# Rotary embedding on one core: the pieces of a tile dealt to the partitions in another order

## The chip, the core and the metric

The kernel runs on one core of a Trainium2 chip. The metric is the device time of one execution in microseconds (us), lower is better. A core has five engines: TensorE (PE), VectorE (DVE), ScalarE (ACT), GpSimd (POOL) and SyncE (SP). Data moves between the large memory (DRAM) and the on-chip SBUF through 16 DMA engines, which the queues of ACT and SP feed here. SBUF has 128 partitions.

## The reference

`x` is 16 x 512 x 1024 in fp32 (33.5 MB): 16 batches, 512 positions, 16 heads of 64. `cos` and `sin` are 512 x 32, one row for each position.

```python
x = x.reshape(batch, seq, num_heads, head_dim)
x1, x2 = x[..., :half_dim], x[..., half_dim:]
cos, sin = cos[None, :, None, :], sin[None, :, None, :]
rotated = np.concatenate([x1 * cos - x2 * sin, x1 * sin + x2 * cos], axis=-1)
```

Every element of `x` is read once and every element of the output is written once. Each row of 1024 is multiplied by its position's cos, its swapped halves by (-sin, sin), and the two products are added.

## The kernel before

**Tiles.** There are ten. Batches 0, 1, 14 and 15 are "singles" (2 MB: 512 rows, four on each partition, `R1 = 4`), and the other twelve batches go as six "pairs" (4 MB: 1024 rows, eight on each partition, `R2 = 8`). What a partition takes of a tile is one contiguous run of rows, a *piece*: 16 KB in a single, 32 KB in a pair. In a single, partition p holds piece p. In a pair, partition 2s+b holds the piece s of batch b of the pair, so that neighbouring partitions are a batch (2 MB) apart in DRAM. One DMA loads a tile and one stores it, from the same SBUF place: `x_sb` is a ring of 40 rows for each partition (five pairs, 20 MB in all) and results overwrite the input.

**Tables.** The cos and sin tables come in by two small DMAs to `stage`, four positions on each partition. For singles this is the right order as it is: DVE copies cos to PSUM (L264), and ACT writes (-sin, sin) to `s1_sb` (L182, L183). For pairs, partition 2s+b needs the eight positions of piece s. Two matmuls (L208) make that from `stage` with two selection matrices `pick`, which ACT cuts from an identity matrix in one ACTIVATE (L177); ACT writes the pairs' (-sin, sin) to `s2_sb` (L186, L187).

**Queues.** ACT issues all loads (L153): tile 0, the tables (L174), tile 1 and four pairs at once, without a wait, and the remaining four when the stores that free their place in the ring have landed. SP issues a store (L161) when the last row of a tile is done.

**Rows.** Each of the 64 rows u of a partition (1024 elements) is worked on in turn. GpSimd multiplies the swapped row by sin into `t2_sb` (L257; for six rows DVE does it, L286). DVE multiplies the row by cos into PSUM, `t1_ps` (L293). Then either DVE adds the two to `x_sb` (L304), or PE adds the product in PSUM with an identity matmul (L224) and ACT copies the sum to `x_sb` (L191), as a fixed list (`PE2`) says. Semaphores count rows: `sem_p` GpSimd's products, `sem_m` DVE's, `sem_v` and `sem_a` finished rows. The first GpSimd multiply waits for `s1_sb` and tile 0; GpSimd's first row of a pair waits for `s2_sb`.

Of the kernel before, what the change touches and what calls it, by code (L numbers as in the profile page):

```python
# [6 lines left out]
def bass_split_heads_rope_kernel(  # L7
# [16 lines left out]
    batch, seq, dim = x.shape  # L24
# [3 lines left out]
    P = 128  # L28
    R1 = seq // P
    R2 = 2 * R1  # L30
    assert R1 * P == seq and R1 == 4 and batch % 2 == 0

    fp32 = mybir.dt.float32
# [3 lines left out]
    COPY = mybir.ActivationFunctionType.Copy  # L37
# [9 lines left out]
    EARLY = (NU - RING) // R2  # L47
# [20 lines left out]
    with ExitStack() as stack:  # L68
        x_sb = stack.enter_context(nc.sbuf_tensor([P, RING, H, 2, HALF], fp32))
        t2_sb = stack.enter_context(nc.sbuf_tensor([P, NT2, H, 2, HALF], fp32))  # L70
        stage = stack.enter_context(nc.sbuf_tensor([P, 2, R1 * HALF], fp32))
        s1_sb = stack.enter_context(nc.sbuf_tensor([P, R1, 2, HALF], fp32))
        s2_sb = stack.enter_context(nc.sbuf_tensor([P, R2, 2, HALF], fp32))
        ident = stack.enter_context(nc.sbuf_tensor([P, P], fp32))
        pick = stack.enter_context(nc.sbuf_tensor([P, 2, P // 2, 2], fp32))
        zero = stack.enter_context(nc.sbuf_tensor([P, BANK], bf16))
        tab_ps = stack.enter_context(nc.psum_tensor([P, BANK], fp32))
        pair_ps = stack.enter_context(nc.psum_tensor([P, 2, 2, R1, HALF], fp32))
# [1 line left out]
        sem_in = [stack.enter_context(nc.semaphore(f"in{t}")) for t in range(NT)]  # L80
        sem_out = [stack.enter_context(nc.semaphore(f"out{k}")) for k in range(EARLY)]
        sem_rest = stack.enter_context(nc.semaphore("rest"))
# [11 lines left out]
        sem_g = stack.enter_context(nc.semaphore("pick"))  # L94
# [9 lines left out]
        def s_of(t, r):  # L104
            return s1_sb[:, r] if tiles[t][1] == R1 else s2_sb[:, r]

        x1 = x.rearrange("b (s r) d -> b s (r d)", r=R1)
        o1 = out.rearrange("b (s r) h d -> b s (r h d)", r=R1)
        x2 = x.rearrange("b (s r) d -> s b (r d)", r=R2)
        o2 = out.rearrange("b (s r) h d -> s b (r h d)", r=R2)  # L110
        xs = x_sb[:].rearrange("p n h t d -> p n (h t d)")

        def in_dram(single, pairs, t):
            b, n = tiles[t]
            return single[b] if n == R1 else pairs[:, b:b + 2, :]

        def in_sbuf(t):
            b, n = tiles[t]
            k = b * R1 % RING
            return x_sb[:, k:k + n].rearrange("p n h t d -> p (n h t d)")  # L120

        def where(u):
            t, r = rows[u]
            return t, r, u % RING
# [7 lines left out]
        def wait_added(eng, u):  # L132

            if n_pe[u]:
                eng.wait_ge(sem_a, n_pe[u])
            if n_comb[u]:
                eng.wait_ge(sem_v, n_comb[u])
# [10 lines left out]
        def stores_of(k):  # L148

            return sum(b * R1 // R2 == k for b, _ in tiles)  # L150

        def load(eng, t):
            eng.dma_start(in_sbuf(t), in_dram(x1, x2, t)).then_inc(sem_in[t], 16)  # L153

        def on_sync(sp):
            for u in range(NU):
                t, r, k = where(u)
                if r == tiles[t][1] - 1:
                    wait_added(sp, u)
                    k = u // R2  # L160
                    sp.dma_start(in_dram(o1, o2, t), in_sbuf(t)).then_inc(sem_out[k] if k < EARLY else sem_rest, 16)  # L161
            sp.wait_ge(sem_rest, 16 * sum(stores_of(k) for k in range(EARLY, NU // R2)))

        def on_scalar(ae):
            later = {}
            for t, (b, n) in enumerate(tiles):
                if b * R1 + n <= RING:
                    load(ae, t)
                else:

                    later.setdefault((b * R1 - RING) // R2 * R2 + R2 - 1 + LAG, []).append(t)
                if t == 0:
                    for i, (table, sem) in enumerate(((cos, sem_cos), (sin, sem_sin))):
                        ae.dma_start(stage[:, i, :], table.rearrange("(s r) d -> s (r d)", r=R1)).then_inc(sem, 16)  # L174

            ae.wait_ge(sem_i, 2)
            ae.activation(  # L177
                pick[:], ident[:].rearrange("q (s k) -> q k s", k=2)[:, :, :, None].broadcast_to([P, 2, P // 2, 2]), COPY
            ).then_inc(sem_g, 1)
            ae.wait_ge(sem_sin, 16)  # L180
            sv = stage[:, 1, :].rearrange("s (r d) -> s r d", d=HALF)
            ae.activation(s1_sb[:, :, 0, :], sv, COPY, scale=-1.0)  # L182
            ae.activation(s1_sb[:, :, 1, :], sv, COPY).then_inc(sem_s, 1)  # L183
            ae.wait_ge(sem_t, 2)
            s2 = s2_sb[:].rearrange("p (k r) t d -> p k r t d", r=R1)
            ae.activation(s2[:, :, :, 0, :], pair_ps[:, :, 1, :, :], COPY, scale=-1.0)  # L186
            ae.activation(s2[:, :, :, 1, :], pair_ps[:, :, 1, :, :], COPY).then_inc(sem_s, 1)  # L187
            for u in range(NU):
                if PE2[u]:
                    ae.wait_ge(sem_e, n_pe[u])  # L190
                    ae.activation(xs[:, u % RING, :], t1_ps[:, u % NT1, :], COPY).then_inc(sem_a, 1)  # L191
                for t in later.get(u, ()):
                    k = (tiles[t][0] * R1 - RING) // R2
                    ae.wait_ge(sem_out[k], 16 * stores_of(k))
                    load(ae, t)

        def on_tensor(pe):
            pe.wait_ge(sem_z, 1)
            for k in range(NT1):
                for b in range(EH):  # L200
                    pe.matmul(  # L201
                        t1_ps[:, k, b * BANK:(b + 1) * BANK], zero[:, 0:P], zero[:], start=True, stop=True
                    ).then_inc(sem_w, 1)
            pe.wait_ge(sem_g, 1)
            pe.wait_ge(sem_cos, 16)
            pe.wait_ge(sem_sin, 16)
            for k in range(2):
                pe.matmul(  # L208
                    pair_ps[:, k].rearrange("p c r d -> p (c r d)"),
                    pick[:, k].rearrange("q s b -> q (s b)"),  # L210
                    stage[:].rearrange("q c f -> q (c f)"),
                    start=True,
                    stop=True,
                ).then_inc(sem_t, 1)
            for u in range(NU):
                if not PE2[u]:
                    continue
                pe.wait_ge(sem_m, u + 1)

                if not V2[u]:  # L220
                    pe.wait_ge(sem_p, n_pool[u])
                t2 = t2_sb[:, u % NT2, :, :, :].rearrange("p h t d -> p (h t d)")
                for b in range(EH):
                    ins = pe.matmul(  # L224
                        t1_ps[:, u % NT1, b * BANK:(b + 1) * BANK],
                        ident[:],
                        t2[:, b * BANK:(b + 1) * BANK],
                        start=False,
                        stop=True,
                        skip_group_check=True,  # L230
                    )
                ins.then_inc(sem_e, 1)
# [28 lines left out]
        def on_vector(ve):  # L261
# [49 lines left out]
            for u in range(NU + LEAD):  # L311
                if u < NU:
                    mul(u)
                if u >= LEAD and not PE2[u - LEAD]:
                    comb(u - LEAD)

        on_sync(nc.sync)
        on_scalar(nc.scalar)
        on_gpsimd(nc.gpsimd)
        on_tensor(nc.tensor)  # L320
        on_vector(nc.vector)

# [32 lines left out]
```

## Time and profile before

| what | value |
|---|---|
| median of 3 runs | 161.33 us (161.15 to 161.42) |
| span of the profiled execution, first to last instruction | 160.3 us |
| median of the runs less that span | 1.0 us |
| busy: POOL, DVE, PE, ACT | 134.9, 130.3, 72.8, 24.4 us |
| DMA | 67.26 MB, 419 GB/s over the span |
| load and store queues, share of 16 DMA engines' span | 49.6% and 48.9% |
| first load issued; first and last store issued | 0.8; 20.5 and 151.7 us |

The span is what the profile shows of one execution; the time of a run is about 1 us more, which lies around it. "Share of 16 engines" is the summed length of a queue's packets over 16 times the span. A row of a group gives busy time and the mean of one instruction, then the idle time before them and who ended it. ACTq and SPq are the issuing queues of ACT and SP: a DMA's row there is only its issue, and its packets follow later. The trace also records each DMA packet with its queue, start, length and size, but not which of the 16 DMA engines carried it.

### The profile page before, as it was taken

How to read it: one execution, taken by the hardware profiler on the slowest of the kernel's cores; microseconds unless marked ns; L12 is line 12 of the kernel's file. 1: busy time of each engine (PE TensorE's matmuls, PEld its weight loads, DVE VectorE, ACT ScalarE, POOL GpSimd, SP SyncE). 2: the span in 40 equal slices, each digit the busy share in tenths (PEclk: the TensorE clock that was granted, in tenths of full speed). 3: DMA queues.
4: the chain of work that ended last, by engine and by line, in shares of the span. 5: the costliest groups of instructions: out<-in, count | busy, mean ns of one | idle time of the engine just before them, and what ended most of it. 6: DMA issues, size and time to landing. Idle time of an engine off the chain costs nothing.

```text
span 160.3 us, 522 instructions
## 1 busy us (share of the span) xinstructions
PE 72.8 (45%) x94; PEld 24.0 (15%) x94; DVE 130.3 (81%) x117; ACT 24.4 (15%) x27; POOL 134.9 (84%) x64
## 2 busy tenths in 40 slices
PE   6050004478357936660847105489458435850000
PEld 1020002022202211210221002022202111220000
DVE  0069998599989999996999709899889999999500
ACT  0420000203120222022012010201220402040000
POOL 1059999999999999999999999699999999289400
PEclk9955555557755587689687965555555977699555
DMA  5999999999999999999999999999999999999896
GB/s 147 409 441 474 409 450 409 425 429 429 446 429 458 417 411 466 409 433 401 450 433 425 425 409 458 409 433 433 411 429 462 441 417 401 450 441 441 376 450 294
DMA packets 3170, 67.26 MB, mean 419 GB/s; under 512 B 352, under 2 KB 608, under 8 KB 608
## 3 DMA queue, kind: packets, MB, share of 16 engines
q10 hardware_dynamic: 1728, 33.69, 49.6%
q1 hardware_dynamic: 1440, 33.56, 48.9%
q14 instruction: 2, 0.02, 0.0%
HBM read 33.69 MB, written 33.55 MB: 419 GB/s over the span
## 4 chain that ended last, share of the span: by engine, by line
DMA 60%; POOL 13%; DVE 8%; PE 7%; issue 3%; ACT 2%; ACTq 1%; DVEq 0%
DMA x_sb<-in_x_dram 41%; DMA out_dram<-x_sb 18%; POOL t_sb L257 13%; PE t_ps L224 7%; DVE t_ps L293 5%; DVE x_sb L304 3%; ACT x_sb L191 2%; ACTq L153 1%; ACTq L174 1%; DVE t_sb L286 0%; DVEq L303 0%
## 5 line engine op out<-in xcount | busy, mean ns | idle before, releaser
L257 POOL TENSOR_TENSOR t_sb<-x_sb,s_sb 128x1024 f32<-128x1024 f32 x58 | 134.2, 2346 | 14.8 <-ACT s_sb L183 8.5
L224 PE MATMUL t_ps<-t_sb,ident 128*128 128x512 f32 x84 | 68.0, 957 | 63.0 <-DVE t_ps L293 39.2
L293 DVE TENSOR_TENSOR t_ps<-x_sb,pair_ps 128x1024 f32<-128x1024 f32 x48 | 57.7, 1223 | 9.9 <-ACT x_sb L191 9.8
L304 DVE TENSOR_TENSOR x_sb<-t_ps,t_sb 128x1024 f32<-128x1024 f32 x43 | 52.4, 1218 | 2.6 <-POOL t_sb L257 2.6
L224 PEld LDWEIGHTS t_ps<-t_sb,ident 128*128 128x128 f32 x84 | 22.1, 290 | 108.9 <-DVE t_ps L293 74.6
L191 ACT ACTIVATE x_sb<-t_ps 128x1024 f32<-128x1024 f32 x21 | 21.5, 1023 | 109.9 <-PE t_ps L224 96.9
L293 DVE TENSOR_TENSOR t_ps<-x_sb,tab_ps 128x1024 f32<-128x1024 f32 x16 | 19.3, 1222 | 0.1
L286 DVE TENSOR_TENSOR t_sb<-x_sb,tab_ps 128x1024 f32<-128x1024 f32 x6 | 7.3, 1213 | 0.0
L264 DVE COPY tab_ps<-stage 128x128 f32<-128x128 f32 x1 | 0.3, 294 | 7.8 <-DMA stage<-in_cos_dram 7.8
L208 PE MATMUL pair_ps<-stage,pick 128*128 128x256 f32 x4 | 2.0, 667 | 5.4 <-DMA stage<-in_sin_dram 5.4
L201 PE MATMUL t_ps<-zero 128*128 128x512 bf16 x6 | 2.7, 627 | 1.3 <-DVE zero L262 1.3
L208 PEld LDWEIGHTS pair_ps<-stage,pick 128*128 128x128 f32 x4 | 1.2, 324 | 6.4 <-issue 6.3
L177 ACT ACT_TABLE_LOAD x1 | 1.3, 1283 | 5.5 <-issue 5.5
L201 PEld LDWEIGHTS t_ps<-zero 128*128 128x128 bf16 x6 | 0.7, 136 | 2.4 <-DVE zero L262 1.2
L262 DVE MEMSET zero<- 128x256 uint32 x1 | 0.3, 272 | 0.9 <-PEq L337 0.9
L186 ACT ACTIVATE s_sb<-pair_ps 128x256 f32<-128x256 f32 x1 | 0.4, 383 | 1.7 <-PE pair_ps L208 1.7
L182 ACT ACTIVATE s_sb<-stage 128x128 f32<-128x128 f32 x1 | 0.3, 309 | 2.1 <-DMA stage<-in_sin_dram 2.1
L235 POOL MEMSET ident<- 128x128 f32 x1 | 0.2, 204 | 0.3 <-POOLq L337 0.3
L177 ACT ACTIVATE pick<-ident 128x256 f32<-128x256 f32 x1 | 0.4, 416 | 0.0
L187 ACT ACTIVATE s_sb<-pair_ps 128x256 f32<-128x256 f32 x1 | 0.4, 379 | 0.0
L237 POOL TENSOR_SCALAR_AFFINE_SELECT ident<-ident 128x128 f32<-128x128 f32 x1 | 0.3, 292 | 0.1
L337 POOL MEMSET const-float32-0.0<- 128x1 f32 x1 | 0.1, 98 | 0.3 <-issue 0.3
(6 smaller groups left out, 1.0 us busy)
## 6 DMA issues: line engine op xcount, KB each, us to landing
x_sb<-in_x_dram ACTq DMA_DIRECT2D x6, 4096.0 KB, 38.0
out_dram<-x_sb SPq DMA_DIRECT2D x6, 4096.0 KB, 25.0
x_sb<-in_x_dram ACTq DMA_DIRECT2D x4, 2048.0 KB, 22.6
out_dram<-x_sb SPq DMA_DIRECT2D x4, 2048.0 KB, 15.2
stage<-in_cos_dram ACTq DMA_DIRECT2D x1, 64.0 KB, 7.8
stage<-in_sin_dram ACTq DMA_DIRECT2D x1, 64.0 KB, 7.5
```

The costliest lines, as they stand in the source:

```text
L153: eng.dma_start(in_sbuf(t), in_dram(x1, x2, t)).then_inc(sem_in[t], 16)
L174: ae.dma_start(stage[:, i, :], table.rearrange("(s r) d -> s (r d)", r=R1)).then_inc(sem, 16)
L177: ae.activation(pick[:], ident[:].rearrange("q (s k) -> q k s", k=2)[:, :, :, None].broadcast_to([P, 2, P // 2, 2]), COPY).then_inc(sem_g, 1)
L186: ae.activation(s2[:, :, :, 0, :], pair_ps[:, :, 1, :, :], COPY, scale=-1.0)
L191: ae.activation(xs[:, u % RING, :], t1_ps[:, u % NT1, :], COPY).then_inc(sem_a, 1)
L201: pe.matmul(t1_ps[:, k, b * BANK:(b + 1) * BANK], zero[:, 0:P], zero[:], start=True, stop=True).then_inc(sem_w, 1)
L208: pe.matmul(pair_ps[:, k].rearrange("p c r d -> p (c r d)"), pick[:, k].rearrange("q s b -> q (s b)"), stage[:].rearrange("q c f -> q (c f)"),
L224: ins = pe.matmul(t1_ps[:, u % NT1, b * BANK:(b + 1) * BANK], ident[:], t2[:, b * BANK:(b + 1) * BANK], start=False, stop=True, skip_group ...
L257: pl.tensor_tensor(t2_sb[:, u % NT2, :, :, :], swapped(k), over_heads(s_of(t, r)), mult).then_inc(sem_p, 1)
L286: ve.tensor_tensor(t2_sb[:, u % NT2, :, :, :], swapped(k), over_heads(v_ps), mult)
L293: ve.tensor_tensor(t1_ps[:, u % NT1, :].rearrange("p (h d) -> p h d", d=HALF), x_sb[:, k, :, :, :].rearrange("p h t d -> p (h t) d"), c_of ...
L304: ve.tensor_tensor(xs[:, k, :], t1_ps[:, u % NT1, :], t2_sb[:, u % NT2, :, :, :].rearrange("p h t d -> p (h t d)"), add,).then_inc(sem_v, 1)
```

## The change

A tile, single or pair, is now 128 pieces in the order of DRAM, and partition 4g+i holds piece 32i+g (g from 0 to 31, i from 0 to 3). Four neighbouring partitions hold pieces 32 apart (512 KB in a single, 1 MB in a pair); partitions 4 apart hold neighbouring pieces. Loads, stores and the two table loads use this order. The sizes and the number of DMAs and of their pieces don't change. The pairs' tables need other selection matrices: `pick` is cut from the identity by four ACTIVATEs of 64 columns each, and PE waits for all four. All else is the same; the lines below the change move by up to 7 (a load's issue is L154, a table's L175, `pick` L182, GpSimd's multiply L264).

```diff
-        pick = stack.enter_context(nc.sbuf_tensor([P, 2, P // 2, 2], fp32))
+        pick = stack.enter_context(nc.sbuf_tensor([P, 2, P], fp32))
...
-        x1 = x.rearrange("b (s r) d -> b s (r d)", r=R1)
-        o1 = out.rearrange("b (s r) h d -> b s (r h d)", r=R1)
-        x2 = x.rearrange("b (s r) d -> s b (r d)", r=R2)
-        o2 = out.rearrange("b (s r) h d -> s b (r h d)", r=R2)
+        QUADS = P // 4
+        x_rows = x.rearrange("b s d -> (b s) d")
+        o_rows = out.rearrange("b s h d -> (b s) (h d)")
...
-        def in_dram(single, pairs, t):
+        def in_dram(all_rows, t):
             b, n = tiles[t]
-            return single[b] if n == R1 else pairs[:, b:b + 2, :]
+            rows_of = all_rows[b * seq:b * seq + P * n, :]
+            return rows_of.rearrange("(i g r) d -> g i (r d)", g=QUADS, r=n)
...
-            eng.dma_start(in_sbuf(t), in_dram(x1, x2, t)).then_inc(sem_in[t], 16)
+            eng.dma_start(in_sbuf(t), in_dram(x_rows, t)).then_inc(sem_in[t], 16)
...
-                        ae.dma_start(stage[:, i, :], table.rearrange("(s r) d -> s (r d)", r=R1)).then_inc(sem, 16)
+                        ae.dma_start(stage[:, i, :], table.rearrange("(i g r) d -> g i (r d)", g=QUADS, r=R1)).then_inc(sem, 16)
...
-            ae.activation(
-                pick[:], ident[:].rearrange("q (s k) -> q k s", k=2)[:, :, :, None].broadcast_to([P, 2, P // 2, 2]), COPY
-            ).then_inc(sem_g, 1)
+            for k in range(2):
+                for m in range(2):
+                    ae.activation(
+                        pick[:, k].rearrange("q (a f m n) -> q m a f n", a=2, m=2, n=2)[:, m],
+                        ident[:].rearrange("q (f k n a) -> q k a f n", k=2, n=2, a=2)[:, k],
+                        COPY,
+                    ).then_inc(sem_g, 1)
...
-            pe.wait_ge(sem_g, 1)
+            pe.wait_ge(sem_g, 4)
...
-                    pick[:, k].rearrange("q s b -> q (s b)"),
+                    pick[:, k],
```

More of the change, by code (lines that the diff above doesn't have):

```diff
@@ L160, in on_sync @@
                     k = u // R2
-                    sp.dma_start(in_dram(o1, o2, t), in_sbuf(t)).then_inc(sem_out[k] if k < EARLY else sem_rest, 16)
+                    sp.dma_start(in_dram(o_rows, t), in_sbuf(t)).then_inc(sem_out[k] if k < EARLY else sem_rest, 16)
             sp.wait_ge(sem_rest, 16 * sum(stores_of(k) for k in range(EARLY, NU // R2)))
```

## The prediction

> **What bounds the kernel now.** I read the shares of the DMA queues first, then the stretches of the span, the chain that ended last, and the issues.
>
> ```profile
> DMA packets 3170, 67.26 MB, mean 419 GB/s; under 512 B 352, under 2 KB 608, under 8 KB 608
> ...
> q10 hardware_dynamic: 1728, 33.69, 49.6%
> q1 hardware_dynamic: 1440, 33.56, 48.9%
> ```
>
> Loads (q10) and stores (q1) together fill 98.5% of 16 DMA engines over the span. 608 packets are small; the rest are 512 of 16 KB and 768 of 32 KB in each queue, one for each partition of a tile (the trace's record of each packet has queue, start, length and size).
>
> ```profile
> core 0: us, PE busy (x) PEld busy (x) DVE busy (x) ACT busy (x) POOL busy (x), PEclk, DMA share, GB/s
> ...
> 12.00:24.00 12.00, 0.00 (x0) 0.00 (x0) 11.70 (x11) 0.11 (x1) 12.00 (x7) 0.50 1.04 445
> ...
> 60.00:90.00 30.00, 16.77 (x24) 5.12 (x22) 28.46 (x26) 5.12 (x5) 30.00 (x14) 0.79 1.00 429
> ...
> 140.00:156.00 16.00, 2.36 (x5) 0.88 (x4) 10.55 (x10) 2.05 (x2) 9.27 (x4) 0.71 0.99 424
> ```
>
> Loads alone (12 to 24), loads beside stores (60 to 90) and stores alone (140 to 156): the DMA share is about 1 in each (a packet counts where it starts, so a stretch can pass 1). The median 32 KB packet takes 1213 ns in either queue and the median 16 KB packet 611 ns: 27 GB/s for an engine, 432 GB/s for 16. The first packet starts at 1.8 us and the last ends near 160.0. All packet lengths together, divided by 16, give 157.9 us, which is that whole stretch. So the span of 160.3 us is 1.8 before the first packet, 157.9 of packets, 0.6 for engines that don't end together and the last completion. The median of the runs, 161.33, is 1.0 above the span; I keep that 1.0.
>
> ```profile
> 93.45 47.51 DMA x_sb<-in_x_dram
> 140.96 0.07 issue
> 141.02 9.29 POOL t_sb L257 x4
> ...
> 150.40 1.23 DVE x_sb L304
> ```
>
> The chain ends on arithmetic, which misleads: the last store is issued at 151.70, but the packets of the store before it run until 155.1. The compute tail has some 2.5 us to spare (3.4 less 0.34 for the issue and 0.6 to a first packet). Packets decide.
>
> Where could the packets be shorter? Against 611 and 1213 ns, the lengths above sum to 27.7 us of engine time, 1.73 us for each engine: 0.74 in the first 1.5 us of loading (18 packets of 16 KB took 831 to 1865 ns), and 0.99 in scattered 32 KB packets of up to 1.57 us while loads and stores run together. Loads alone after the start, and the stores from 140 on, have none.
>
> **The change part by part.** (1) The bytes, packet counts and sizes stay: each partition still gets one run of 16 or 32 KB in every transfer, 512 bytes in a table. 157.9 less 1.73, or 156.2 us, therefore stays.
>
> (2) The DRAM side of the four single loads, four single stores and two tables becomes a list in two steps, 32 by 4, where it was one run of 128. The pair tiles have a list in two steps already, 64 by 2, so their rows price it.
>
> ```profile
> 0.81 0.37 ACTq L153 DMA_DIRECT2D x_sb<-in_x_dram  x1
> 1.21 0.46 ACTq L174 DMA_DIRECT2D stage<-in_cos_dram  x1
> 1.69 0.45 ACTq L174 DMA_DIRECT2D stage<-in_sin_dram  x1
> ...
> 53.60 0.54 ACTq L153 DMA_DIRECT2D x_sb<-in_x_dram  x1
> ```
>
> The first load, a single, is issued in 0.37 us; a pair load on an ACT queue that isn't full takes 0.54. Difference 0.17 us. Only this first issue is exposed, since nothing moves before it: today's first packet starts 0.64 us after its end. The bounds are 0 (packets may be released before the issue ends) and 0.29 (the slowest pair issue on this queue, 0.66, less 0.37). I take 0.17, the row nearest in kind. All other issues lie under full queues: two tables and a second single of at most 0.2 more each, on ACT, shift ACT's first computing instruction from 5.5 to about 6.1; four single stores on SP, 0.34 to 0.54, wait behind packets.
>
> (3) One ACTIVATE that builds `pick` becomes four of 128x64 with stepped operands.
>
> ```profile
> L177 ACT ACTIVATE pick<-ident 128x256 f32<-128x256 f32 x1 | 0.4, 416 | 0.0
> L182 ACT ACTIVATE s_sb<-stage 128x128 f32<-128x128 f32 x1 | 0.3, 309 | 2.1 <-DMA stage<-in_sin_dram 2.1
> ```
>
> From 416 and 309 ns a 128x64 would take about 255; four make 1.02, 0.6 more than now (1.25 more if each took 416). ACT waits 2.08 us for the sin table behind it, which holds 0.6 of issues and 0.6 of activations, and even 0.6 with 1.25. Cost: nothing. PE now waits for four counts, with the pair-table matmuls behind; they start when sin lands, at 9.37, while the last `pick` would be done by 8.5. If that cover went, GpSimd's first multiply (9.85) and so the first store (20.48) would be late, and still loads fill the engines to beyond 50 us: six loads, 21 MB at 432 GB/s, are issued by 5.4 us.
>
> (4) What each instant touches in DRAM. Singles: neighbouring partitions were 16 KB apart and become 512 KB apart, pieces four partitions apart go from 64 KB to 16 KB. Pairs: neighbours were 2 MB apart (one batch each), become 1 MB apart; four partitions apart, 64 KB becomes 32 KB. This is the unknown, and the trace has only neighbours of it. Its bounds: below, all 1.73 us of stretched packets vanish; above, the stretch doubles, +1.73. The nearest rows say zero: the pair tiles, with neighbours 2 MB apart, have the same price per byte (1213 ns for twice the bytes of 611) as singles in one run, so the engines' own rate and not the memory sets a packet's length. I take 0.
>
> A rule of the Trainium skill speaks against the change: DMA: Bandwidth & Descriptors, section Latency and other measured facts, has copies of 128 rows of 16 KB at 207 GB/s each way for a row pitch of 512 KiB, 164 for 2 MiB, and 214 where the pitch is padded. Read for neighbouring partitions this would stretch 156 us by at least 3%, an estimate of +5 us. The row here disagrees for pitches that alternate over two places, as the pair tiles' 2 MB does; none shows four places.
>
> Also unknown: the engines end 0.5 us apart from their mean (the slowest against the average of 16, from the packets' ends). Another order can move that by 0.5 either way; I take 0.
>
> Sum: 161.33 + 0.17 + 0 + 0 + 0 = 161.5 us, 0.1% over.
>
> **The rivals.** *Forecast: neutral.* The memory pattern doesn't show, the issue costs its 0.17, the unequal ends give a few tenths: 161.1 to 161.9.
>
> *Faster: the packets' stretch goes.* At the start 16 engines begin within 0.45 us, by step four 64 KB apart; if they meet in the same part of the memory, 16 KB apart they may not. Without the start's stretch: 161.33 + 0.17 − 0.74 = 160.8. Without any: 161.33 + 0.17 − 1.73 = 159.8. For it: the stretched packets are there, and bunch where all engines start or reads meet writes. Against: a first access may be slow wherever it goes, and loads alone (12 to 24 us) have no stretch with 64 KB steps.
>
> *Slower: four places.* Each run of four partitions jumps by 512 KB or 1 MB. If that makes the pieces meet in the memory, reads beside writes suffer first, as they hold the stretch of today. Twice today's stretch gives 161.33 + 0.17 + 1.73 = 163.2. It decides the sign from an added stretch of about 0.15 us for each engine on (that and 0.17 pass 0.32), some 3 ns on each 32 KB packet. For it: such stretches exist. Against: the pair tiles' unhurt 2 MB.
>
> *The change does nothing.* If DMA engines take pieces in an order unrelated to partitions, only 0.17 is left: inside the neutral case.
>
> **How the numbers follow.** A measurement of this kernel tells about 0.2%, 0.32 us, from no change: 161.01 to 161.65 is the same. Neutral has 0.45, of which 0.27 falls within, 0.14 above (unequal ends on top of the issue) and 0.04 below. The gain has 0.26, the loss 0.29, because the changed issue already stands on its side. Faster 0.30, same 0.27, slower 0.43. The likeliest case alone is 161.1 to 161.9; the range for 8 in 10 takes in nearly all of the gain (160.0) and the loss to its doubled stretch (163.2), and leaves out a loss by the rule's size.
>
> **What would show it.** Right: medians of 1213 and 611 ns as before, the queues' shares again summing to 98 to 99% of a span within 0.5 us of 160.3, a first L154 issue of about 0.54 us with the first packet near 2.0 us, four `pick` ACTIVATEs done before sin lands, the first GpSimd multiply still near 9.9. Gain: no packets above 800 ns at the start. Loss: longer packets in stretches where loads meet stores, and GB/s below 425 there. Wrong in another way: a DMA share under 0.95 in a middle stretch, which would mean that the engines ran dry.

## The result, and the profile after

The changed kernel takes 167.24 us in the median of 6 runs (166.16 to 170.23), the one before 161.31 (161.10 to 161.61, 6 runs). The ratio is 1.0334, with a 95% interval of 1.0316 to 1.0351: slower by 5.4 us on that ratio, where the prediction had 161.5 and at most 163.2. The ratios leave out executions more than 1.5% above the fastest of their kernel (two of the six here, 168.96 and 170.23 us, and of the kernel before two of 78, at 168.66 and 163.68 us), and no reading below rests on a profile of one.

The profiled execution after, the fastest of the six, has a span of 164.7 us, 4.4 more than before. The queues' part of its page:

```profile
DMA packets 3170, 67.26 MB, mean 408 GB/s; under 512 B 352, under 2 KB 608, under 8 KB 608
...
q10 hardware_dynamic: 1728, 33.69, 48.5%
q1 hardware_dynamic: 1440, 33.56, 48.2%
```

Packets and bytes are the same. The two queues fill 96.7% of 16 DMA engines' span instead of 98.5%, so some engines idled somewhere. The stretches of the span say where (columns: us, busy time of PE, PEld, DVE, ACT and POOL, granted clock, DMA share, GB/s):

```profile
12.00:24.00 12.00, 0.00 (x0) 0.00 (x0) 12.00 (x11) 0.00 (x0) 12.00 (x6) 0.50 1.05 440
60.00:90.00 30.00, 17.51 (x22) 5.51 (x21) 27.19 (x25) 5.12 (x5) 30.00 (x14) 0.67 1.00 426
110.00:140.00 30.00, 18.05 (x23) 5.82 (x23) 29.17 (x27) 5.12 (x5) 27.55 (x12) 0.67 1.00 418
140.00:156.00 16.00, 3.15 (x6) 0.68 (x4) 11.66 (x10) 2.05 (x2) 9.26 (x4) 0.71 0.93 398
```

The third stretch was, before:

```profile
110.00:140.00 30.00, 18.07 (x23) 5.48 (x21) 29.13 (x26) 5.12 (x5) 26.52 (x12) 0.67 1.00 427
```

Up to 140 us the DMA engines are as full as before, at little less GB/s (426 and 418; before 429 and 427). From 140 on the share is 0.93 where it was 0.99. Here is the end of the chain of work that ended last (start, length, what):

```profile
134.83 4.67 POOL t_sb L264 x2
139.50 5.80 another core or an unknown queue
145.30 0.07 issue
145.37 9.27 POOL t_sb L264 x4
154.64 0.03 issue
154.67 0.02 DVEq L310
154.69 0.04 issue
154.73 1.23 DVE x_sb L311
```

GpSimd stands still for 5.8 us before the last tile (the chain doesn't name what released it). What it waits for is in the waits (us in total, times, longest), after and before:

```profile
POOL t_sb L264 <- DMA x_sb<-in_x_dram: 8.0, 3, 5.9
```

```profile
POOL t_sb L257 <- DMA x_sb<-in_x_dram: 4.3, 2, 3.9
```

It is the last load: the longest wait for a load is 5.9 us, and 3.9 before. The kernel takes a load as landed when its semaphore has counted to 16, and the packet records show 16 writes of 4 bytes for each load, which I read as one from each DMA engine (its completion). Of the last load, the median one comes at 139.3 us (139.7 before) and the last at 145.0 (140.5 before). So the typical DMA engine is as early as it was, and the slowest is 4.4 us later; that is the whole difference of the spans. A few of the 16 lag, and more from load to load: the fourth-last is complete 2.3 us after its median (at 92.5 us), the third-last 3.8 (at 113.6, with four completions more than 3 us late), the second-last 5.3, the last 5.6. A slow engine is also the end: the last store's last completion comes at 164.4, the median one at 162.2.

The lag comes from stretched packets, but not from their mean. All stretch together (length beyond 1213 or 611 ns) is 3.12 us for each engine, 1.73 before; the median packets are unchanged. Between 75 and 140 us, 95 packets of pair stores are stretched by over 100 ns, 19 before. An engine can be followed although the records don't name it, since a packet mostly starts 3 or 4 ns before the end of the one ahead of it. Followed back from the last completion of the last load, where a tie with another engine can't always be excluded, the engine takes a load and a store in turn, and nine of its ten pair stores from 118 to 137 us are 138 to 292 ns too long, 1.8 us together.

### The profile page after: what moved, and what is told of

It is laid out like the page before. It is cut to its first block, busy times and chain, and to the rows that moved or that the text cites. A ratio compares the mean times of both kernels' runs of the same rounds, so it can differ in the third digit from the quotient of the medians.

```text
span 164.7 us, 525 instructions
## 1 busy us (share of the span) xinstructions
PE 72.4 (44%) x94; PEld 23.4 (14%) x94; DVE 130.4 (79%) x117; ACT 24.6 (15%) x30; POOL 134.9 (82%) x64
## 4 chain that ended last, share of the span: by engine, by line
DMA 51%; POOL 27%; PE 5%; another core or an unknown queue 4%; DVE 3%; issue 2%; ACTq 1%; ACT 1%; DVEq 0%
DMA x_sb<-in_x_dram 35%; POOL t_sb L264 27%; DMA out_dram<-x_sb 16%; PE t_ps L231 5%; DVE t_ps L300 2%; ACT x_sb L198 1%; DVE x_sb L311 1%; ACTq L175 1%; ACTq L154 1%; DVEq L310 0%
## 5 line engine op out<-in xcount | busy, mean ns | idle before, releaser
L264 POOL TENSOR_TENSOR t_sb<-x_sb,s_sb 128x1024 f32<-128x1024 f32 x58 | 134.2, 2349 | 19.1 <-ACT s_sb L190 8.2
L231 PEld LDWEIGHTS t_ps<-t_sb,ident 128*128 128x128 f32 x84 | 21.5, 282 | 110.5 <-DVE t_ps L300 76.9
L182 ACT ACTIVATE pick<-ident 128x64 f32<-128x64 f32 x4 | 0.7, 248 | 0.0
```

The lines of the kernel that those rows point to most:

```text
L182: ae.activation(pick[:, k].rearrange("q (a f m n) -> q m a f n", a=2, m=2, n=2)[:, m], ident[:].rearrange("q (f k n a) -> q k a f n", k=2, ...
L231: ins = pe.matmul(t1_ps[:, u % NT1, b * BANK:(b + 1) * BANK], ident[:], t2[:, b * BANK:(b + 1) * BANK], start=False, stop=True, skip_group ...
L264: pl.tensor_tensor(t2_sb[:, u % NT2, :, :, :], swapped(k), over_heads(s_of(t, r)), mult).then_inc(sem_p, 1)
```

## Experiments

### Which DMAs do it

Four kernels deal only one part. Each is the changed kernel with another `in_dram` for the rest; here is the second:

```diff
-            return rows_of.rearrange("(i g r) d -> g i (r d)", g=QUADS, r=n)
+            if n == R1:
+                return rows_of.rearrange("(g r) d -> g (r d)", r=n)
+            return rows_of.rearrange("(i g r) d -> g i (r d)", g=QUADS, r=n)
...
-    table.rearrange("(i g r) d -> g i (r d)", g=QUADS, r=R1)
+    table.rearrange("(s r) d -> s (r d)", r=R1)
```

Singles alone dealt:

> Only the singles (and the tables) are dealt over four places; pairs lie as before. Theory A (the pair tiles' four places 1 MB apart make a few DMA engines lag): as before, 161.3 to 161.7 us, the 16 completions of the last load within 2.6 us of each other. Rival B (the dealt singles at the start set the DMA engines against each other and the lag then only grows): as the changed kernel, 165 to 167 us, with completions of the last load 5 us or more apart. Rival C (loads and stores must be dealt alike for it): between, as the four 2 MB stores and loads are a quarter of the bytes, 162 to 163 us.

Measured: 1.0057 (1.0038 to 1.0076), with the five runs at 161.97, 162.00, 162.51, 168.36 and 169.56 us. Theory A wanted no change and B 1.03; by the ratio neither holds, and two runs were longer than B's 167.

Pairs alone dealt:

> Only the pairs are dealt over four places; singles and tables lie as before, so the first load's issue is back at 0.37 us. Theory A (pair tiles' four places make a few DMA engines lag): 166 to 168 us, completions of the last load 5 us or more apart. Rival B (the singles set it off): 161.3 to 162 us, completions within 2.6 us.

Measured: 1.0023 (0.9994 to 1.0052), span 159.7 us. Theory A falls: the pairs' four places, three quarters of the bytes, cost nothing that can be told, and the 16 completions of the last load end at 139.9, 0.4 us after their median.

Loads alone dealt:

> All loads and the tables are dealt, the stores lie as before, so that the output's rows stand in another order. Loads of pairs held 0.46 us of the 1.39 us of stretch for each engine that the change added, stores of pairs 0.99. Theory A1 (each direction adds by itself): +1.5 to +2 us over before, 162.8 to 163.4 us. Theory A2 (stores alone are hurt): 161.3 to 161.8 us. Rival C (an engine's load and store of the same places have to meet): 161.3 to 161.8 us here and in the run with dealt stores as well.

Measured: 1.0070 (1.0049 to 1.0092), between theories A1 and A2, with the four runs at 162.27, 162.48, 166.16 and 169.46 us.

Stores alone dealt:

> All stores are dealt, the loads and tables lie as before, so that the output's rows stand in another order. Theory A1 (each direction adds by itself): +3.5 to +4 us over before, 164.8 to 165.3 us. Theory A2 (stores alone are hurt): 166 to 168 us. Rival C (load and store of the same places have to meet): 161.3 to 161.8 us.

Measured: 1.0343 (1.0262 to 1.0424), as much as the whole change, and theory A2 by the ratios. Dealt stores are enough for the loss, and since dealt pairs are harmless, the stores of singles came under suspicion, or a meeting of both kinds. (The spread of the runs with dealt loads says that loads may start it too.)

The next four split the stores. The edit is a flag (`dealt`) for each load and store, as in the second of them:

```diff
-    sp.dma_start(in_dram(o_rows, t), in_sbuf(t))
+    sp.dma_start(in_dram(o_rows, t, tiles[t][1] == R1), in_sbuf(t))
```

Stores of pairs alone dealt:

> Only the six stores of pairs are dealt; loads, tables and the stores of singles lie as before (the output's rows of pairs stand in another order). Dealing all stores gave 1.034 of before. Theory D (pair stores by themselves are slow in four places): 1.03 or more, 166 us, with the last load's completions 4 us or more apart. Theory E (the stores of singles, beside the first loads of pairs, set the DMA engines apart, and only then do pair stores lag): 1.00 to 1.003, 161.2 to 161.7 us.

Measured: 0.9998 (0.9984 to 1.0012). Theory D falls.

Stores of singles alone dealt:

> Only the four stores of singles are dealt, all else lies as before (the output's rows of singles stand in another order). Theory D (pair stores by themselves): 1.000 to 1.002, 161.2 to 161.5 us. Theory E (the stores of singles set it off): 1.02 or more, 164.5 us, with completions of the last load 4 us or more apart.

Measured: 1.026 (1.0202 to 1.0319). Four stores of 2 MB, an eighth of all bytes, are enough for most of the loss.

All dealt but the stores of singles:

> The changed kernel with the stores of singles as before (the output's rows of singles stand in another order). Theory D: still 1.03, 166 us. Theory E: 1.004 to 1.008, 162 to 162.5 us, of which 0.4 us is the later first packet.

Measured: 163.25 to 169.96 us in four runs, with no interval; before ran 161.07 to 161.43 beside it. Even the fastest is 1.2% over, more than theory E allowed: something else can set the lag off as well. Its trace, of that fastest run, has the first store issued at 20.88 us, 0.4 later than before, which becomes telling below.

All dealt but the loads of singles and the tables:

> The changed kernel with the loads of singles and the tables as before (data of singles not matched to the order of the stores), so that the first packet is back at 1.83 us from 2.20. Theories D and E: as the changed kernel less 0.4 us, 1.03, 166 us. Theory F (the start decides: dealt singles let the DMA engines start in step, and the lag grows from there): 1.000 to 1.003, as with dealt pairs alone.

Measured: 1.0325 (1.0291 to 1.0359). The later start isn't the cause: the first packet is back at 1.8 us, and the last load's completions still reach from a median of 138.4 to 146.1. Theory F falls. In this trace nearly all the stretch from 95 to 136 us is in single packets of pair stores, from 115 us on 2 us apart (at 115, 117, 119, 121, 123 us and so on, 100 to 400 ns each), as they would come from one engine that takes a load and a store in turn.

### Which stores, and what about them

The first two stores of singles alone dealt (`t < 2`):

> Of the four stores of singles only the first two (tiles 0 and 1, from 20 us on, beside loads of pairs) are dealt; all else as before (their rows stand in another order). Dealing all four gave 1.026. Theory E1 (the first two put one or a few DMA engines behind the others, and those engines' later stores of pairs are then stretched): 1.02 or more, 164.5 us. Theory E2 (the last two matter, at the end where nothing follows to even it out): 1.000 to 1.003.

Measured: 1.0317 (1.0263 to 1.0370). Two stores, issued at 20 and 31 us, do as much as the whole change.

The last two alone (`t >= NT - 2`):

> Only the last two stores of singles (issued after 143 us) are dealt; all else as before. Theory E1: 1.000 to 1.002, 161.2 to 161.5 us. Theory E2: 1.02 or more.

Measured: 1.0007 (0.9990 to 1.0024). The same kind of store, at the end, costs nothing.

Two places instead of four:

> The four stores of singles in two places instead of four: partition 2g+i stores to piece 64i+g, neighbours 1 MB apart, partitions four apart 32 KB apart; the issue is a list of 64 by 2, 0.54 us or more as with four places (their rows stand in another order). Theory G (a list in two steps is issued and served later, which puts the DMA engines out of step): 1.02 or more, as with four places. Theory H (what counts is the addresses: 512 KB between neighbours, 16 KB between engines): 1.000 to 1.005.

Measured: 1.0410 (1.0353 to 1.0467). Not the 512 KB between places, then, nor the 16 KB between engines; and the first store's issue took 0.63 us here too.

The first two stores later by a row, in the kernel before:

```diff
-    wait_added(sp, u)
+    wait_added(sp, u + 1 if t < 2 else u)
```

> The kernel before, with the stores of tiles 0 and 1 waiting for one row more, so that each is issued one row (some 2.3 us) later; all addresses as before. Theory G (only when the first stores enter among the loads matters): 1.01 or more, with the last load's completions more than 4 us apart. Theory H (addresses): 1.000 to 1.002, 161.2 to 161.5 us, since the DMA engines have loads to do until beyond 50 us.

Measured: 1.0000 (0.9989 to 1.0011). I read this as the end of theory G, too early, as the last two runs show.

Addresses without a second step: the two stores woven into each other at twice the pitch.

```diff
+    o_first = out[0:2].rearrange("b s h d -> (b s) (h d)").rearrange("(p t r) d -> p t (r d)", t=2, r=R1)
...
+    if t < 2:
+        dst = o_first[:, t, :]
```

> The kernel before, with the stores of tiles 0 and 1 woven into each other: piece p of tile t goes to place 2p+t of the first 4 MB (their rows stand in another order). The DRAM side stays a list of one step, 128 pieces at a pitch of 32 KB instead of 16 KB, so only addresses change. Theory H (the addresses of these two stores make DMA engines lag): 1.02 or more. Theory L (the list in two steps does, whatever the addresses): 1.000 to 1.003, first store issued in 0.38 us.

Measured: 0.9996 (0.9980 to 1.0011).

A second step without other addresses: pieces in order, a gap of 4 KB after every fourth.

```diff
+    spare = nc.dram_tensor("spare", [2, P // 4, 4 * R1 + 1, dim], fp32, kind="Internal").ap()
...
+    return spare[t, :, 0:4 * R1, :].rearrange("g (i r) d -> g i (r d)", r=R1)
```

> The kernel before, with the stores of tiles 0 and 1 going to a spare DRAM tensor (so these two batches are left out of the output): pieces in order, with a gap of 4 KB after every fourth, which makes it a list of 32 by 4 with nearly the addresses of before. Theory L (the list in two steps): 1.02 or more, 164.5 us or more, the first store issued in 0.63 us. Theory H (addresses): 1.000 to 1.003.

Measured: 1.0234 (1.0181 to 1.0287).

Its control, the same tensor without gaps:

> The control of the run with the list in order: tiles 0 and 1 stored to the same spare tensor without gaps, as a list of one step. Both theories: 1.000 to 1.003. If it is 1.02 or more, the spare tensor itself disturbs and the other run says nothing of lists.

Measured: 0.9995 (0.9979 to 1.0011). The three together: the order in DRAM is not needed for the loss, and a two-step list, with small gaps, is enough for it. The issue of the first store, from the timelines of the kernel before, of the one without gaps and of the one with gaps (start, length, queue, line):

```profile
20.48 0.38 SPq L161 DMA_DIRECT2D out_dram<-x_sb  x1
```

```profile
20.24 0.33 SPq L170 DMA_DIRECT2D spare<-x_sb  x1
```

```profile
20.22 0.60 SPq L169 DMA_DIRECT2D spare<-x_sb  x1
```

The list takes 0.27 us longer to issue. In the packet records the first packet of the store starts at 23.9, 23.9 and 24.1 us.

More bytes for two DMA engines (16 KB from each of two partitions, twice):

```diff
+    if t == 0:
+        for j in range(2):
+            sp.dma_start(spare[2 * j:2 * j + 2, :], in_sbuf(t)[0:2, :]).then_inc(sem_x, 16)
```

> The kernel before, with two more DMAs on the SP queue ahead of the first store: each writes 16 KB from partitions 0 and 1 to a spare tensor, so that (if two partitions go to two DMA engines) two DMA engines get 1.2 us more to do than the others; all else as before. Theory M (a DMA engine that is behind the others gets its later packets stretched, so a lag grows): 1.02 or more, the last load's completions 4 us or more apart. Rival N (a lag stays as it is): 161.3 to 162.6 us, that is at most the 1.2 us given, with the last load's completions 2.5 to 4 us apart.

Measured: 1.0117 (1.0077 to 1.0158), with the last load's completions at 136.5 (median) to 140.2. Between the two theories, and the extra issues also made the first store later by 0.9 us; the last two runs separate that.

### When the first store's packets come in

One tiny DMA ahead of the first store, in the kernel before:

```diff
+    if t == 0:
+        for j in range(1):
+            sp.dma_start(spare[2 * j:2 * j + 2, 0:16], in_sbuf(t)[0:2, 0:16]).then_inc(sem_x, 16)
```

> The kernel before, with one tiny DMA (2 x 64 bytes to a spare tensor) on the SP queue ahead of the first store, so that this store, one step as before, is issued some 0.3 us later; a list in two steps takes 0.26 us longer to issue. Theory P (when the first store's packets enter among the loads decides, and 0.3 us is enough to miss a turn of 1.2 us): 1.01 or more. Theory L (something in a list of two steps itself): 1.000 to 1.003.

Measured: 1.0369 (1.0321 to 1.0418). All addresses and all large DMAs are those of before. The store's issue in its timeline:

```profile
20.30 0.32 SPq L166 DMA_DIRECT2D spare<-x_sb  x1
...
20.68 0.48 SPq L167 DMA_DIRECT2D out_dram<-x_sb  x1
```

The store's issue begins 0.2 us later than before and ends 0.3 us later (21.16 against 20.86), and its first packet starts at 24.4 instead of 23.9. The end of its chain and its wait for loads are those of the changed kernel:

```profile
141.79 5.61 another core or an unknown queue
147.41 0.07 issue
147.47 9.27 POOL t_sb L264 x4
```

```profile
POOL t_sb L264 <- DMA x_sb<-in_x_dram: 12.2, 4, 5.7
```

Two tiny DMAs:

> The same with two tiny DMAs (some 0.55 us later), which is the run that put two DMA engines behind without the bytes that put them behind. Theory M (the 1.2 us given to two DMA engines made that run 1.0117): 1.000 to 1.003 here. Theory P (its later first store did): 1.01 or more here as well.

Measured: 1.0068 (1.0048 to 1.0088). So the loss doesn't grow with the delay: a first packet 0.5 us later gives 1.037, 1.1 us later 1.007, and 2.3 us later nothing. Against this control the two engines put behind cost 163.21 less 162.41, or 0.8 us, no more than the 1.2 they were given. That speaks against theory M, that a lag grows merely because it is there; the control isn't exact, since its first store is issued at 21.02 us and the other's at 21.41.

The traces side by side, from the packet records: when the first packet of the first store starts, the 16 completions of the last load, and two counts. "Ahead" is how many 16 KB store packets start before the first gap of more than 0.45 us in such starts (each is the first of its engine); "late" is how many engines complete the last load more than 3 us after the median.

| kernel | ratio | first packet, us | last load: median, last, us | ahead | late |
|---|---|---|---|---|---|
| before | | 23.9 | 139.7, 140.5 | 8 | 0 |
| pairs dealt | 1.0023 | 23.8 | 139.5, 139.9 | 14 | 0 |
| pair stores dealt | 0.9998 | 23.8 | 139.3, 139.9 | 15 | 0 |
| last two dealt | 1.0007 | 23.9 | 139.5, 139.9 | 13 | 0 |
| one step, woven | 0.9996 | 23.8 | 139.5, 139.9 | 15 | 0 |
| one step, spare tensor | 0.9995 | 23.9 | 139.6, 139.9 | 13 | 0 |
| two-step list in order | 1.0234 | 24.1 | 138.6, 144.9 | 4 | 4 |
| two places | 1.0410 | 24.1 | 138.7, 144.8 | 4 | 4 |
| first two dealt | 1.0317 | 24.2 | 138.9, 144.3 | 2 | 2 |
| all but loads of singles | 1.0325 | 24.4 | 138.4, 146.1 | 1 | 1 |
| changed kernel | 1.0334 | 24.4 | 139.3, 145.0 | 5 | 5 |
| one tiny DMA | 1.0369 | 24.4 | 138.9, 147.0 | 1 | 1 |
| two tiny DMAs | 1.0068 | 25.0 | 138.2, 139.4 | 7 | 0 |
| a row later | 1.0000 | 26.2 | 136.9, 137.5 | 10 | 0 |

Where the first packet comes at 23.8 to 23.9 nothing is lost, and where it comes at 24.1 to 24.4 one to five engines lag by up to 5 to 8 us at the last load. All but the stores of singles (24.3, completions to 142.1) belongs to the second group: its stores are in one step, but late. A load packet of 32 KB takes 1.21 us, so 25.0 and 26.2 are one and two packets after 23.85, and 24.1 to 24.4 a fifth to a half of one: the place within a packet seems to count.

The two counts say how. The engines end their load packets at different moments (before, a load completes on one engine after another from 22.4 to 23.3 us), so the moment at which store packets come in decides how many engines turn to a store at once and how many first take another load. Where only one to five go ahead, the same number is late at the end; where seven or more do, the latest is at most 1.2 us behind. With one tiny DMA the late engine can be followed back: it is the one whose store began first, at 24.41 us, and not one of the two that carried the tiny packets at 23.94 and 23.95. The changed kernel's five began at 24.42 to 24.55, the next one at 25.34. These counts were read from the traces afterwards, and no run was made to try them. All but the stores of singles has no such gap in its starts and doesn't fit so neatly. Singles alone dealt and loads alone dealt have no profile that belongs in the table.

Why engines that go ahead in small numbers fall behind, which of the 16 they are by number, and why their packets of pair stores are then stretched, stays open. No version beat the kernel before: the best ones are within their intervals of 1.

## Why the prediction was wrong

**What bounds the kernel.** That packets decide was right, and that bytes, packet counts and median packets stay (1). But I added packet lengths over 16 engines and took their mean as the clock. A load lands when the slowest engine has written, and the end is the slowest engine's end. The mean rose by 1.39 us of stretch and 0.38 of start; the slowest engine rose by 4.4. The 1.0 us around the span is 1.5 here (166.16 less 164.7). It set the median of three runs against the span of another execution; in every run that has both on record, of any kernel, time and span lie 1.4 to 1.5 us apart.

**The step that failed is in (2):** "All other issues lie under full queues", with the stores of singles going from 0.34 to 0.54. The longer issue was seen rightly and priced at nothing, because SP's queue has time. Its cost is not time on SP: what it can move is the moment at which store packets enter among the loads. The issue of the first store went from 0.38 to 0.64 us:

```profile
20.16 0.64 SPq L162 DMA_DIRECT2D out_dram<-x_sb  x1
```

The first two stores alone, dealt, cost 3.2%; pieces in order with a list in two steps (1.0234, control 0.9995) show that a list in two steps is enough, and one tiny DMA ahead of that store in the kernel before (1.0369) shows that a shift of half a microsecond with a list in one step is enough too. That the list acts through the shift alone is argued from the table, not shown: no run has a list in two steps with its first packet at 23.9 us. In the changed kernel the issue itself even ends 0.06 us earlier than before (20.80 against 20.86, as GpSimd began 0.3 us sooner), and the first packet still starts 0.5 us later (24.4 against 23.9).

**The first load's issue** was mis-sized: I took 0.17, with 0 to 0.29 as bounds.

```profile
0.81 0.60 ACTq L154 DMA_DIRECT2D x_sb<-in_x_dram  x1
...
1.43 0.62 ACTq L175 DMA_DIRECT2D stage<-in_cos_dram  x1
...
2.08 0.62 ACTq L175 DMA_DIRECT2D stage<-in_sin_dram  x1
```

It takes 0.60, 0.23 more, and the first packet starts at 2.20 instead of 1.82, 0.38 later: another 0.15 passes between the issue's end and the first packet. The row I took (0.54) came from a queue that had been idle; the pair loads at the start, 0.57 to 0.66, were nearer in kind.

**`pick`** (3) cost nothing, as worked out:

```profile
L182 ACT ACTIVATE pick<-ident 128x64 f32<-128x64 f32 x4 | 0.7, 248 | 0.0
...
L189 ACT ACTIVATE s_sb<-stage 128x128 f32<-128x128 f32 x1 | 0.3, 309 | 0.9 <-DMA stage<-in_sin_dram 0.9
```

Four of 248 ns, 0.71 us with their overlap, and ACT still waits 0.9 us for sin. GpSimd's first multiply is at 9.5, before at 9.9.

**The memory pattern** (4) at 0 was right for pairs (stores 0.9998; loads and stores 1.0023) and for addresses alone (0.9996). The start's stretch even fell from 0.74 to 0.48 us, as the "faster" rival wanted, and it was worth nothing. (That rival let the 16 engines begin within 0.45 us; in the packet records of before eleven do, and fifteen within 0.8. And 0.15 us over an engine's 96 packets of 32 KB is 1.6 ns for each, not the 3 of the "slower" rival.) The rival "slower: four places" had the sign, and the wrong mechanism: two places lose 4.1%, and pieces in order 2.3%. The rule of the Trainium skill (DMA: Bandwidth & Descriptors, section Latency and other measured facts) on row pitches gave +5 us by estimate, close to the measured 5.4. The closeness is luck: with 1 MB between the pairs' pieces nothing is lost, while a two-step list with its pieces in order loses 2.3%.

**The unequal ends** were bounded by 0.5 us either way, from a single trace in which the engines happened to end together. That is the second step that failed, and it holds the whole loss: 0.9 us from the median to the last completion of the last load became 5.6. The tail's cover of 2.5 us was right as arithmetic, and 4.4 us of late load used it up: the median completion of the last store comes 2.6 us later (162.2 against 159.6). The end itself is the slowest engine's, by its own packets: the store before has its last completion at 159.5 (155.1 before), and eight packets of 0.61 us from there end at the 164.4 of the last.

## What to carry to other kernels

Where DMA packets fill the span, the limit is the slowest of the 16 DMA engines, not their sum: read the spread of a transfer's completions, and give any change of its moment or form a bound of several per cent, not of the mean. A DMA issue hidden under a full queue need not be free, since it still decides when its packets come in among others. Before explaining such a loss by addresses, run the old addresses with the issue shifted by a few tenths of a microsecond.

## What the runs showed of the hardware

A store whose DRAM side is a list in two steps took 0.53 to 0.65 us to issue, one in a single step 0.32 to 0.38 (0.48 and 0.56 straight behind small DMAs). The first load took 0.60 with a list in two steps and 0.37 in one, and its first packet came 0.38 us later. A first store whose first packet came 0.5 us later, behind one tiny DMA, made the same kernel 3.7% slower, while 2.3 us later made no difference. One to five of the 16 DMA engines fell up to 5 to 8 us behind the others within some 120 us at unchanged median packets; in each of those traces the gap at the last load is larger than at any load before.
